# Splitting f32 weights three half units ahead, with four split buffers and three raw ones, in a one-core decoder layer

## The chip, the cores and the metric

The kernel runs on one core of a Trainium2 chip. The time is the device time of one execution in microseconds (us); the figure that counts is the median over several executions of the same kernel. The core has five engines with an instruction queue each: PE (TensorE matmul; its weight loads are listed apart as PEld), DVE (VectorE), ACT (ScalarE), POOL (GpSimd) and SP (SyncE, which here only issues transfers). They meet through semaphores. The profile gives the clock that TensorE was granted in each stretch as a share of full speed.

## What is computed

One layer of a hybrid decoder on a prompt of 2048 tokens and 8 sample tokens, width 1024, all in f32. Cut to what matters here:

```
h   = rmsnorm(x) @ w_in                     # 1024 x 3592, then two recurrent mixers side by side
o   = concat(gated_delta_net(h), mlstm(h))  # 4 + 4 heads, chunkwise, 2048 x 1024
x   = x + rmsnorm(o @ w_out)                # 1024 x 1024
u   = square(relu(rmsnorm(x) @ w_up))       # 1024 x 4096
y   = x + rmsnorm(u @ w_down)               # 4096 x 1024
```

The outputs are y for the prompt and for the sample tokens, and the states of the mixers.

## The kernel before

The prompt is worked through in four segments of 512 tokens, called 0 to 3 here; the 8 sample tokens ride with segment 1, whose tiles are therefore 520 columns wide and are multiplied in two pieces of 260. Within a segment the four weight matrices come one after another: w_in, w_o (the output projection, `w_out` above), w_up, w_dn. Each product of f32 numbers is made from three products of parts: weights and activations are each split into a high part of fewer bits and the remainder, and PE multiplies high by high (line 195), high by the activations' low part (line 196) and low by high (line 200).

A **half unit** (class `Half`, from line 155; "half" below) is one weight tile of 128 rows and 512 columns, 256 KB in HBM, that covers half of the summed dimension of one 128-wide block of outputs. For a segment's 512 columns it takes 12 matmuls. Before PE can start, the tile must be in SBUF and split:

- `load` (lines 167 to 171) takes a raw buffer, `wraw`, from a ring of four and issues the transfer on SP's queue. The buffer comes free when the subtraction of its earlier tile is done.
- `split` (lines 173 to 183) takes a buffer, `whl`, from a ring of three; ACT casts the raw tile into its first half (the high part, line 178) and DVE subtracts (line 183) to leave the low part in its second half. The buffer comes free when PE has done its last matmul on the earlier tile.
- `go` (lines 185 to 203) issues the matmuls.

There are 880 halves. In the w_o stage the columns of a segment are taken in two groups of 256, so each weight tile is loaded and split twice, and a half there is half as long on PE: 32 halves for each segment. These stages lie at about 413 to 471 us (segment 0), 1079 to 1137 (segment 1), 1716 to 1766 (segment 2) and 2193 to 2250 (segment 3).

`play` (lines 1358 to 1390) walks the list of halves. Before it issues half n it issues loads and splits that run ahead of it: all splits below n + 2, and before each split all loads below that split's number + 4. The splits are put at high priority. Between halves it lets background work run a piece at a time: the mixers (the gated delta net, its output scaling, transposes and store at lines 695 to 704, decay factors at 493 and 496; the mLSTM from line 708, decay at 730), `b_prep` (lines 1090 to 1102, which fetches the mixers' output `dO` from HBM again as `xt` and splits it into X, line 1101 on ACT, 1102 on DVE), and `norm_mid` (lines 1192 to 1220, the norm after w_o: scale with the gain at 1214, residual sum at 1215, high part of X on ACT at 1217, low part on DVE at 1218). norm_mid of a segment runs behind that segment's w_o stage, beside the matmuls of the next stage; POOL takes every second of its sums at 1215 and sums of squares at 1141. A scheduler then sets the order of each engine's queue by these priorities and by its own estimates, so a change of a number in `play` can move instructions of every engine.

Of the kernel before, what the change touches and what calls it, by code (L numbers as in the profile page):

```python
# [12 lines left out]
F32R = mybir.dt.float32r  # L13
# [11 lines left out]
def program(tc, ctx, d, T):  # L25
# [14 lines left out]
    def sb(shape, tag, bufs=1, dt=F32):  # L40
        return wk.tile(shape, dt, tag=tag, name=tag, bufs=bufs)
# [44 lines left out]
    w0 = []  # L86
    gain = const([128, 4, 8], "gain")
    for tt, tag in enumerate(("xt", "xt", "qk", "qk")):
        if tt == 2:
            Q.dma_start(gain, d["gains"])  # L90
            for i in range(2):
                w0.append(sb([128, 512], "wraw", 4))
                Q.dma_start(w0[i], d["w_gate"][:, i * 512:(i + 1) * 512])
        t = sb([128, 1040], tag, 2)
        Q.dma_start(t[:, :1024], d["x_prompt"][tt * 128:(tt + 1) * 128])
        x0.append(t)
        xs0.append(big[:, tt * 1024:(tt + 1) * 1024] if tt < 2 else sb([128, 1040], "xs", 3)[:, :1024])
# [48 lines left out]
    def tok(s, tt):  # L146
        return (tt * 128, 128) if tt < 4 else (SEG, NB)
# [9 lines left out]
    class Half:  # L157
# [9 lines left out]
        def load(self):  # L167
            if self.same is not None or self.raw is not None:
                return
            self.raw = sb([128, 512], "wraw", 4)  # L170
            Q.dma_start(self.raw, self.src)

        def split(self):
            if self.same is not None:
                self.hl = self.same.hl
                return
            self.hl = sb([128, 2, 512], "whl", 3, F32R) if self.keep is None else self.keep()
            A.copy(self.hl[:, 0], self.raw)  # L178
            raw, hi, lo = self.raw[:, :], self.hl[:, 0], self.hl[:, 1]
            if self.packed:  # L180
                raw, hi = (t.rearrange("p (a b) -> p a b", b=32)[:, :, 4:8] for t in (raw, hi))
                lo = hi
            V.tensor_tensor(lo, raw, hi.bitcast(F32), op=ALU.subtract)  # L183
# [991 lines left out]
    def pairs(src, c0, c1, tag="xt"):  # L1175

        w = c1 - c0
        k = 4 if 4 * w <= 1040 else 2

        def load(j):  # L1180
            t = sb([128, 1040], tag, 3 if tag == "xs" else 2)[:, :k * w].rearrange("p (a b) -> p a b", a=k)
            Q.dma_start(t, src[j:j + k, :, c0:c1].rearrange("j p t -> p j t"))
            return t
        ahead = load(0)
        for j in range(0, 8, k):
            t, ahead = ahead, load(j + k) if j + k < 8 else None
            yield j, k, t
# [153 lines left out]
    def step():  # L1341
        r = next(streams[0], "end")
        if r == "end":
            streams.pop(0)
            return 0.0
        return float(r or 1)
# [11 lines left out]
    def play():  # L1358
        halves = []
        for it in main:  # L1360
            h = it[0] if isinstance(it, tuple) else it
            if isinstance(h, Half) and h not in halves[-4:]:
                halves.append(h)
        place = {id(h): i for i, h in enumerate(halves)}
        loaded = split = 0
        for it in main:
            h, part = it if isinstance(it, tuple) else (it, None)
            if not isinstance(h, Half):
                it()
                continue  # L1370
            n = place[id(h)]
            while split < min(n + 2, len(halves)):
                while loaded < min(split + 4, len(halves)):
                    halves[loaded].load()
                    loaded += 1
                with tc.high_priority(300):
                    halves[split].split()
                split += 1
            while loaded < min(split + 4, len(halves)):
                halves[loaded].load()  # L1380
                loaded += 1
            h.go(part)
            if streams:
                state["due"] += h.cost() * state["rate"]
                while streams and state["due"] > 0:
                    state["due"] -= step()
            else:
                state["due"] = 0.0
# [6 lines left out]
    for group in groups(tts(0)):  # L1395
        rows = []
        for tt in group:
            n = tok(0, tt)[1]
# [115 lines left out]
    main.append(lambda: stream(final(last, 256, width(last), sumss[last], FAST, True)))  # L1514
    main.append(flush)
    play()


# [72 lines left out]
```

## Time and profile before

| | |
|---|---|
| median of 3 executions | 2653.05 us (2652.44 to 2653.79) |
| the profiled execution | 2654.11 us |
| its span in the profile | 2652.3 us |
| PE busy | 2599.9 us, 98% of the span |
| DVE, ACT, POOL busy | 1727.5, 1283.5, 433.3 us |
| moved by transfers | 377.40 MB, 142 GB/s on average |

PE is busy nearly throughout, so the time is the sum of PE's work and of the moments in which PE has nothing ready. The views that show those are the waits of PE (what ended its idle time, summed), the timeline of PE (each group of like instructions with the idle time ahead of it) and the windows (busy time, granted clock and transfer rate of a stretch).

### The profile page before, as it was taken

What the parts mean: (1) busy time and instruction counts of PE and PEld (TensorE: products, weight loads), DVE (VectorE), ACT (ScalarE), POOL (GpSimd) and SP (SyncE); (2) the same over time, 40 slices, a digit from 0 to 9 for tenths busy, and PEclk for the clock granted to TensorE, in tenths of its full rate; (3) what the DMA queues carried; (4) which work ended last, traced back from release to release, by engine and by line L of the source; (5) the groups of instructions that cost most, each with busy time, mean ns of one, the idle gap of its engine ahead of it and who ended that gap; (6) DMA issues with size and microseconds to landing.
All of it is one profiled execution on the core that took longest, in us unless ns stands there. A gap on an engine that the chain in (4) does not pass through costs nothing.

```text
span 2652.3 us, 44344 instructions
## 1 busy us (share of the span) xinstructions
PE 2599.9 (98%) x15912; PEld 2268.5 (86%) x15912; DVE 1727.5 (65%) x3513; ACT 1283.5 (48%) x3120; POOL 433.3 (16%) x494
## 2 busy tenths in 40 slices
PE   8999999999999999999999999999999999999998
PEld 6879999787888788878899999997787888788887
DVE  7665758647747656774775766577758566765445
ACT  5636557435536345653655444466354355433332
POOL 2101112311000000530100000054000003552002
PEclk9999999999999999999999999999999999999999
DMA  5444457654324345754433343455333346565222
GB/s 173 155 147 144 151 152 222 207 156 134 108 92 126 96 141 167 236 186 135 139 97 110 107 141 119 138 173 163 99 112 112 106 144 205 182 197 147 93 96 84
DMA packets 292221, 377.40 MB, mean 142 GB/s; under 512 B 42325, under 2 KB 147785, under 8 KB 291993
## 3 DMA queue, kind: packets, MB, share of 16 engines
q1 hardware_dynamic: 289312, 365.13, 44.2%
q0 software_dynamic: 2688, 9.44, 1.3%
q8 instruction: 126, 2.06, 0.3%
q14 instruction: 95, 0.77, 0.1%
HBM read 314.04 MB, written 60.53 MB: 141 GB/s over the span
## 4 chain that ended last, share of the span: by engine, by line
PE 88%; DVE 4%; DMA 4%; issue 2%; ACT 1%; POOL 0%; SPq 0%; DVEq 0%; ACTq 0%; POOLq 0%
PE bk L195 26%; PE bk L196 26%; PE bk L200 26%; DMA wraw<-w_o 1%; DVE whl L183 1%; DVE nt L1214 1%; DMA xt<-x_prompt 1%; DVE X L1218 1%; DMA xt<-dO 1%; PE mx L563 1%; PE mx L655 1%; PE mx L770 1%; PE mx L680 1%; PE mx L681 1%; PE mx L747 1%
## 5 line engine op out<-in xcount | busy, mean ns | idle before, releaser
L178 ACT CAST whl<-wraw 128x512 fp32r<-128x512 f32 x872 | 539.4, 620 | 933.7 <-PE bk L200 866.3
L183 DVE TENSOR_TENSOR whl<-wraw,whl 128x512 fp32r<-128x512 f32 (+1 forms) x872 | 636.3, 732 | 447.5 <-ACT whl L178 433.3
L195 PE MATMUL bk<-Y,whl 128*128 128x512 f32 (+2 forms) x2208 | 733.9, 347 | 4.2 <-ACT whl L178 2.0
L196 PE MATMUL bk<-Y,whl 128*128 128x512 f32 (+2 forms) x2208 | 732.1, 346 | 0.0
L195 PE MATMUL bk<-X,whl 128*128 128x512 f32 (+3 forms) x2024 | 654.9, 340 | 7.2 <-ACT whl L178 7.1
L196 PE MATMUL bk<-X,whl 128*128 128x512 f32 (+3 forms) x2024 | 653.5, 339 | 2.7 <-DVE X L1218 2.5
L200 PE MATMUL bk<-Y,whl 128*128 128x512 f32 (+2 forms) x2176 | 488.2, 344 | 6.9 <-DVE whl L183 6.9
L195 PEld LDWEIGHTS bk<-Y,whl 128*128 128x128 f32 x2208 | 416.2, 189 | 58.9 <-ACT whl L178 3.4
L196 PEld LDWEIGHTS bk<-Y,whl 128*128 128x128 f32 x2208 | 416.9, 189 | 50.4
L200 PE MATMUL bk<-X,whl 128*128 128x512 f32 (+3 forms) x2024 | 442.4, 339 | 8.9 <-DVE whl L183 8.8
L195 PEld LDWEIGHTS bk<-X,whl 128*128 128x128 f32 x2024 | 381.8, 189 | 50.5 <-ACT whl L178 9.5
L196 PEld LDWEIGHTS bk<-X,whl 128*128 128x128 f32 x2024 | 381.7, 189 | 47.5 <-DVE X L1218 4.1
L200 PEld LDWEIGHTS bk<-Y,whl 128*128 128x128 f32 x2176 | 359.1, 189 | 59.5 <-DVE whl L183 8.6
L200 PEld LDWEIGHTS bk<-X,whl 128*128 128x128 f32 x2024 | 326.3, 188 | 54.3 <-DVE whl L183 11.5
L1262 DVE TENSOR_TENSOR acc<-acc,bk 128x512 f32<-128x512 f32 (+2 forms) x296 | 164.3, 557 | 157.3 <-PE bk L200 153.4
L1141 POOL TENSOR_TENSOR NQ<-NQ,nt 128x256 f32<-128x256 f32 (+4 forms) x145 | 143.3, 991 | 470.5 <-ACT nt L1140 464.1
L1251 DVE TENSOR_TENSOR tB<-tB 128x512 f32<-128x512 f32 (+1 forms) x160 | 96.9, 608 | 44.1 <-ACT Y L1250 43.1
L305 DVE SCALAR_TENSOR_TENSOR tB<-tA,cw,tB 128x512 f32<-128x512 f32 x144 | 108.0, 750 | 13.6 <-ACT tB L301 9.3
L1252 DVE TENSOR_TENSOR Y<-tB,Y 128x512 fp32r<-128x512 f32 (+1 forms) x160 | 98.0, 615 | 3.2
L596 DVE TENSOR_TENSOR W<-xt 32x30 f32<-32x30 f32 (+14 forms) x240 | 76.2, 317 | 22.3 <-DMA xt<-dn 17.5
L1249 ACT ACTIVATE tB<-bk 128x512 f32<-128x512 f32 (+1 forms) x160 | 81.8, 511 | 16.1 <-PE bk L200 13.0
L1250 ACT ACTIVATE Y<-tB 128x512 fp32r<-128x512 f32 (+1 forms) x160 | 87.2, 549 | 4.3
(397 smaller groups left out, 2481.8 us busy)
## 6 DMA issues: line engine op xcount, KB each, us to landing
wraw<-w_dn SPq DMA_DIRECT2D x264, 256.0 KB, 2.8
wraw<-w_up SPq DMA_DIRECT2D x256, 256.0 KB, 2.8
wraw<-w_a SPq DMA_DIRECT2D x224, 256.0 KB, 2.9
wraw<-w_o SPq DMA_DIRECT2D x128, 256.0 KB, 3.3
dqkv<-tB SPq DMA_DIRECT2D x48, 256.0 KB, 3.3
gb<-drb SPq DMA_DIRECT2D x32, 256.0 KB, 3.8
qk<-dqkv SPq DMA_DIRECT2D x16, 512.0 KB, 5.7
dzo<-tB SPq DMA_DIRECT2D x32, 256.0 KB, 3.3
```

Of the source, the lines that this page charges most:

```text
L178: A.copy(self.hl[:, 0], self.raw)
L183: V.tensor_tensor(lo, raw, hi.bitcast(F32), op=ALU.subtract)
L195: PE.matmul(o, lhsT=w, rhs=acts[:, k, 0, c0:c1], start=(self.first and k == 0), stop=False)
L196: PE.matmul(o, lhsT=w, rhs=acts[:, k, 1, c0:c1], start=False, stop=(self.packed and self.last and k == 3))
L200: PE.matmul(o, lhsT=w, rhs=acts[:, k, 0, c0:c1], start=False, stop=(self.last and k == 3))
L305: V.scalar_tensor_tensor(acc, pre[:, t:t + SEG], cw[:, j, t:t + 1], acc, op0=ALU.mult, op1=ALU.add)
L1141: G.tensor_tensor(total[:, c0:c1], total[:, c0:c1], sq[:, c0:c1], op=ALU.add)
L1249: A.activation(r[:, :n], p[:, :n], AF.Relu)
L1250: A.activation(sl[:, 0, c0:c1], r[:, :n], AF.Square)
L1251: V.tensor_tensor(r[:, :n], r[:, :n], r[:, :n], op=ALU.mult)
L1252: V.tensor_tensor(sl[:, 1, c0:c1], r[:, :n], sl[:, 0, c0:c1].bitcast(F32), op=ALU.subtract)
L1262: V.tensor_tensor(a, a, p[:, :c1 - c0], op=ALU.add)
```

## The change

Three numbers change. The ring of `wraw` has three buffers instead of four, the ring of `whl` four instead of three, and `play` keeps splits below n + 3 instead of n + 2, with loads below split + 3 instead of split + 4. So the farthest load ahead of half n stays at n + 6, the farthest split goes from half n + 1 to n + 2, and the raw tiles that wait between load and split are one fewer. A raw buffer has 2 KB per partition, a split one 4 KB.

```
-                w0.append(sb([128, 512], "wraw", 4))
+                w0.append(sb([128, 512], "wraw", 3))
...
-            self.raw = sb([128, 512], "wraw", 4)
+            self.raw = sb([128, 512], "wraw", 3)
...
-            self.hl = sb([128, 2, 512], "whl", 3, F32R) if self.keep is None else self.keep()
+            self.hl = sb([128, 2, 512], "whl", 4, F32R) if self.keep is None else self.keep()
...
-            while split < min(n + 2, len(halves)):
-                while loaded < min(split + 4, len(halves)):
+            while split < min(n + 3, len(halves)):
+                while loaded < min(split + 3, len(halves)):
...
-            while loaded < min(split + 4, len(halves)):
+            while loaded < min(split + 3, len(halves)):
```

What it does to the queues is seen at two places. The first is DVE's queue behind segment 1's w_o stage, where norm_mid of segment 1 (lines 1214, 1215, 1218, 520 columns wide) stands between the subtractions of the weight tiles (line 183). Before:

```order
L183 TENSOR_TENSOR whl<-wraw,whl 128x512
L1214 SCALAR_TENSOR_TENSOR nt<-acc,gain,NQ 128x520 x3
L1218 SCALAR_TENSOR_TENSOR X_10967<-acc,gain,X_10967 128x520 x2
L1215 TENSOR_TENSOR acc<-nt,xt 128x520
L1218 SCALAR_TENSOR_TENSOR X_10967<-acc,gain,X_10967 128x520
L1214 SCALAR_TENSOR_TENSOR nt<-acc,gain,NQ 128x520
L183 TENSOR_TENSOR whl<-wraw,whl 128x512
L1218 SCALAR_TENSOR_TENSOR X_10967<-acc,gain,X_10967 128x520
L1214 SCALAR_TENSOR_TENSOR nt<-acc,gain,NQ 128x520
L183 TENSOR_TENSOR whl<-wraw,whl 128x512
L1218 SCALAR_TENSOR_TENSOR X_10968<-acc,gain,X_10968 128x520 x2
L1215 TENSOR_TENSOR acc<-nt,xt 128x520
```

And with the change:

```order
L183 TENSOR_TENSOR whl<-wraw,whl 128x512
L1214 SCALAR_TENSOR_TENSOR nt<-acc,gain,NQ 128x520 x2
L1218 SCALAR_TENSOR_TENSOR X_10970<-acc,gain,X_10970 128x520 x3
L1214 SCALAR_TENSOR_TENSOR nt<-acc,gain,NQ 128x520
L1215 TENSOR_TENSOR acc<-nt,xt 128x520
L183 TENSOR_TENSOR whl<-wraw,whl 128x512
L1218 SCALAR_TENSOR_TENSOR X_10970<-acc,gain,X_10970 128x520
L1214 SCALAR_TENSOR_TENSOR nt<-acc,gain,NQ 128x520
L183 TENSOR_TENSOR whl<-wraw,whl 128x512
L1218 SCALAR_TENSOR_TENSOR X_10971<-acc,gain,X_10971 128x520
L1215 TENSOR_TENSOR acc<-nt,xt 128x520
L1218 SCALAR_TENSOR_TENSOR X_10971<-acc,gain,X_10971 128x520
```

The runs of norm work between two subtractions stay about as long; each subtraction stands about one place further on, so the one for a given half (half 385, for instance) has 15 of the norm's operations ahead of it where it had 18.

The second place is ACT's queue at about 268 us, in segment 0's mixers, where a cast (line 178) stands ahead of the delta net's decay factors, which wait for POOL (line 496), and the next one behind them. Before:

```order
L178 CAST whl<-wraw 128x512
L345 COPY samp<-bk 128x8
L300 COPY tA<-bk 128x252
L301 ACTIVATE tB<-bk,cw 128x252
L496 ACTIVATE E<-E,iF 128x128 x4
L730 ACTIVATE gb<-gb,mp_112 128x128
L178 CAST whl<-wraw 128x512
L730 ACTIVATE gb<-gb,mp_112 128x128 x3
```

And with the change:

```order
L178 CAST whl<-wraw 128x512
L345 COPY samp<-bk 128x8
L300 COPY tA<-bk 128x252
L301 ACTIVATE tB<-bk,cw 128x252
L331 ACTIVATE tB<-bk 128x260
L496 ACTIVATE E<-E,iF 128x128 x4
L178 CAST whl<-wraw 128x512
L730 ACTIVATE gb<-gb,mp_112 128x128 x4
```

The rows read nearly alike, but the cast ahead of line 496 is that of half 77 instead of half 76, and the one behind it that of half 78 instead of 77.

Two more facts of the order are used below. In segment 3 the rows of DVE around its last L703 are the same word for word, each subtraction belonging to the next half. And in segment 0's w_o stage PE meets the last four transposes of the mixers' output (line 702) six halves later, in half 128 instead of 122, so that five halves instead of ten stand between them and the first matmul (half 133) that reads the columns of X made from them.

## Rows read from the trace of the kernel before

**Rows 1.** The page: the span, and busy time of each engine.

```profile
span 2652.3 us, 44344 instructions
...
PE 2599.9 (98%) x15912; PEld 2268.5 (86%) x15912; DVE 1727.5 (65%) x3513; ACT 1283.5 (48%) x3120; POOL 433.3 (16%) x494
```

**Rows 2.** Waits of PE: line waited for, us in total, times, longest us.

```profile
PE bk L200 <- DVE whl L183: 15.7, 14, 2.7
PE bk L195 <- ACT whl L178: 9.1, 12, 1.4
```

**Rows 3.** Timeline of PE: start us, us, group, [idle before, who ended it].

```profile
268.33 0.39 PE L195 MATMUL bk<-Y,whl 128*128 128x260 f32 x1 [1.35 <-ACT whl L178]
...
501.36 1.19 PE L200 MATMUL bk<-Y,whl 128*128 128x512 f32 x4 [1.03 <-DVE whl L183]
...
507.03 1.20 PE L200 MATMUL bk<-Y,whl 128*128 128x512 f32 x4 [2.62 <-DVE whl L183]
...
1173.82 1.54 PE L200 MATMUL bk<-Y,whl 128*128 128x512 f32 x4 [2.69 <-DVE whl L183]
...
1759.83 0.74 PE L200 MATMUL bk<-X,whl 128*128 128x256 f32 x4 [1.43 <-DVE whl L183]
...
2200.47 0.75 PE L200 MATMUL bk<-X,whl 128*128 128x256 f32 x4 [2.63 <-DVE whl L183]
```

**Rows 4.** Timeline of ACT at 268 us.

```profile
266.20 1.28 ACT L496 ACTIVATE E<-E,iF 128x128 f32<-128x128 f32 x4 [5.02 <-POOL E L493]
267.68 0.60 ACT L178 CAST whl<-wraw 128x512 fp32r<-128x512 f32 x1
```

**Rows 5.** Timeline of DVE in norm_mid of segment 1.

```profile
1163.67 0.75 DVE L1214 SCALAR_TENSOR_TENSOR nt<-acc,gain,NQ 128x520 f32<-128x520 f32 x1
1164.94 1.80 DVE L1218 SCALAR_TENSOR_TENSOR X<-acc,gain,X 128x520 fp32r<-128x520 f32 x1
...
1173.08 0.68 DVE L183 TENSOR_TENSOR whl<-wraw,whl 128x512 fp32r<-128x512 f32 x1
```

**Rows 6.** Timeline of DVE in segment 3's w_o stage.

```profile
2199.07 0.75 DVE L703 SCALAR_TENSOR_TENSOR on<-mx,ghalf,on 128x512 f32<-128x512 f32 x1 [4.85 <-DMA wraw<-w_o]
2199.73 1.89 DVE L183 TENSOR_TENSOR whl<-wraw,whl 128x512 fp32r<-128x512 f32 x3
```

**Rows 7.** Window: us, busy PE, PEld, DVE, ACT, POOL; clock, DMA share, GB/s.

```profile
1170.00:1180.00 10.00, 7.13 (x24) 4.87 (x23) 9.59 (x8) 6.14 (x12) 7.69 (x6) 0.83 0.45 141
```

**Rows 8.** Timeline of ACT, then DVE, in segment 2's w_o stage, undisturbed.

```profile
1723.27 0.62 ACT L178 CAST whl<-wraw 128x512 fp32r<-128x512 f32 x1 [0.23 <-PE bk L200]
1724.67 0.62 ACT L178 CAST whl<-wraw 128x512 fp32r<-128x512 f32 x1 [0.78 <-PE bk L200]
...
1723.92 0.69 DVE L183 TENSOR_TENSOR whl<-wraw,whl 128x512 fp32r<-128x512 f32 x1 [0.71 <-ACT whl L178]
```

**Rows 9.** Windows of the w_o stages of segments 0, 1 and 3 (columns as rows 7).

```profile
413.00:471.00 58.00, 56.30 (x480) 55.35 (x479) 48.70 (x140) 43.04 (x120) 14.99 (x18) 1.00 0.74 226
1079.00:1137.00 58.00, 53.05 (x427) 51.08 (x426) 46.87 (x74) 39.77 (x91) 30.90 (x35) 1.00 0.78 250
...
2193.00:2250.00 57.00, 50.39 (x398) 48.72 (x397) 36.49 (x55) 33.36 (x79) 18.18 (x20) 0.97 0.71 212
```

**Rows 10.** Tile `wraw`, issue to landing, in the windows of rows 9, in order.

```profile
DMA to landing us min/median/max: 3.2/4.5/4.9
...
DMA to landing us min/median/max: 3.3/5.0/6.1
...
DMA to landing us min/median/max: 2.8/3.6/5.4
```

**Rows 11.** Waits of ACT for late weight tiles (columns as rows 2).

```profile
ACT whl L178 <- DMA wraw<-w_o: 24.0, 14, 3.6
```

**Rows 12.** Timeline of DVE, end of segment 0's mixers.

```profile
426.29 0.75 DVE L703 SCALAR_TENSOR_TENSOR on<-mx,ghalf,on 128x512 f32<-128x512 f32 x1 [0.47 <-PE mx L702]
...
434.12 0.69 DVE L1102 TENSOR_TENSOR X<-xt,X 128x512 fp32r<-128x512 f32 x1 [1.13 <-ACT X L1101]
```

## Prediction

> **What bounds the kernel now.** The page comes first: PE is busy for 2599.9 of the span's 2652.3 us [rows 1], so at most 52.4 us can be had from anything but less work on PE. The waits of PE come next, since the change touches one thing on PE's side, how early a split tile is ready: 15.7 us for the low parts from DVE and 9.1 us for the high parts from ACT, 24.8 us together [rows 2]. The rest of PE's idle time waits for norms and other matters that stay. The timeline of PE then shows where the 24.8 us lie [rows 3]: few and long stalls, not many short ones. Those I price are at 268 us (segment 0's mixers), 501 and 507 us (norm_mid of segment 0), 1174 us (norm_mid of segment 1), 1760 us (norm_mid of segment 2; one like it, 1.44 us, stands at 2244 us in segment 3), and 2200 us. All profiled figures belong to the execution of 2654.11 us, 1.8 us longer than its span and 1.06 us above the median of 2653.05; I take the sum off the median. A difference under 0.2%, 5.3 us, can't be told from none.
>
> **Why these stalls can shrink.** In each, the tile had long been in SBUF and its split stood behind something else on the queue of ACT or DVE. At 268 us the cast stood behind the decay factors, which had waited 5.02 us for POOL, and began at 267.68 [rows 4]. In norm_mid of segment 1 the subtraction began at 1173.08, behind a run of the norm's operations that take 1.80 us where the like of them take 0.75 in other moments [rows 5], and PE's next matmul on a low part began at 1173.82. At 2200 us DVE stood 4.85 us, in front of the scaling at L703, and then did three subtractions in a row [rows 6]. The change doesn't shorten these queues; it moves each split one half further ahead of PE, so PE has one half more to work on when the queue stops. A half's worth is 1.40 us at 256 columns, which is the step from one cast to the next where nothing disturbs [rows 8], and twice that, 2.8 us, at 512.
>
> **The gains.** Each stall can shrink by at most itself or one half's worth, and by nothing if the queue's delay grows with the lead. The stall at 268: 1.35 us, under one half's 2.8, and the cast that stood behind L496 now stands ahead of it: -1.35 (0 to -1.35). At 501 and 507, 1.03 + 2.62 = 3.65 us is one delay met twice: -2.0 (0 to -2.8), since DVE's queue carries the same work either way. At 1174, 2.69 us: -2.4 (0 to -2.7). At 1760 and 2244, 1.43 and 1.44 us, halves now of 256 columns and then 512: -1.0 each, -2.0 (0 to -2.8). At 2200, 2.63 us against 1.40: -1.3 (0 to -1.4). Sum -9.05 (0 to -11.1). The other waits in the 24.8 us (at the start, and short ones in the w_o stages, behind transfers) I leave as they are.
>
> **The clock.** Behind three of these stalls, at 507, 1174 and 2200 us, the granted clock averages 0.83 over 10 us; the window behind the second stands for the three [rows 7]. That is 3.4 us at 1.2 instead of 2.4 GHz, and every such dip costs 0.17 x 10 = 1.7 us of PE's work on top of the stall. A dip that follows a stall may go when the stall shrinks. I take two of three, as the gains above leave 0.3 us of the stall at 1174, 1.3 of that at 2200 and 1.65 of the pair at 501 and 507: -3.4 (0 to -5.1).
>
> **The price: three raw buffers.** A raw buffer is held from the issue of its load to the end of its subtraction: landing, then cast and subtraction, which undisturbed take from 1723.27 to 1723.92 + 0.69, 1.34 us [rows 8]; I take 1.4 with the reissue. With landing L, four buffers feed a half each (L + 1.4)/4 us, three (L + 1.4)/3. In w_a, w_up and w_dn a half takes PE 2.8 us, three of them 8.4 us, well over any landing seen, so the ring costs nothing there. The w_o stages are the place, with halves of 256 columns; there SP issues as soon as a buffer is freed. From rows 9 and 10, by the median landing:
>
> - segment 0: (4.5 + 1.4)/3 = 1.97 us against the stage's pace of 58/32 = 1.81: 32 x 0.16 = +5.1
> - segment 1: (5.0 + 1.4)/3 = 2.13 against 1.81: 32 x 0.32 = +10.2
> - segment 3: (3.6 + 1.4)/3 = 1.67 against 57/32 = 1.78: nothing; segment 2, whose landings are shorter, nothing either.
>
> With four buffers the same four sums give 1.48, 1.60 and 1.25, always under the pace. So the upper bound is +15.3. The lower is 0: the three split tiles ahead of PE absorb late ones, and where the mixers' own matmuls stand between the halves a late tile costs nothing. Which lies nearer? ACT already waits 24.0 us for late w_o tiles [rows 11], while all of PE's waits for ACT's casts are 9.1 us [rows 2]: 0.38 of the lateness at most comes through. 0.38 x 15.3 = **+5.8**.
>
> **The moved transposes.** In segment 0 PE meets the mixers' last four transposes six halves later, so five halves instead of ten lie between them and the first matmul that reads X made from them. From L703 to the end of X's low part took 426.29 to 434.81, 8.5 us [rows 12], by way of a store and a fetch. Five halves of 256 columns are 5 x 1.40 = 7.0 us and about 0.7 for the transposes; 0.8 us is missing: **+1.0** (0 to +2.8, if the landings there lengthen by 2 us). The other moves that the order shows (norm_mid of segment 0 begins two halves earlier on PE, the norm before the mixers some halves earlier or later) keep their distance in time to what they feed, and I cost them at nothing.
>
> **The sum.** -9.05 - 3.4 + 5.8 + 1.0 = -5.65, so 2653.05 - 5.65 = **2647.4 us**.
>
> **The rivals.**
>
> 1. Fewer transfers in flight land sooner. In the w_o stages with four loads outstanding the landing is 4.5 and 5.0 us at 226 and 250 GB/s, and 3.6 at 212 [rows 9, 10]. If the time in the queue falls with the number outstanding, L falls by a quarter to 3.4 and 3.75 us, three buffers give 1.6 and 1.72 us, under the pace of 1.81, and the ring's price falls to about +1; with it the +1.0 of the transposes: -9.05 - 3.4 + 1.0 = -11.45, 2641.6 us. For it: landings as short as 2.8 us in the same stages. Against it: the mixers' and norms' own transfers share these stretches and stay. The Trainium skill, "DMA: Bandwidth & Descriptors", section "Latency and other measured facts", has it that a lighter load on HBM makes the fixed cost of a transfer smaller; the three rows, longer landings at higher rates, agree in direction.
>
> 2. DVE is the bound in norm_mid of segments 0 and 1, and a lead of one half is eaten in the stretch. In segment 1 DVE is busy 9.59 us of 10 there and POOL 7.69 [rows 7], and the same operation takes 1.80 instead of 0.75 us [rows 5]. Then the stalls and the dips at 507 and 1174 stay where they were: 2.0 + 2.4 and two thirds of the 3.4, 6.7 us, don't come, and -5.65 + 6.7 = +1.05: 2654.1 us, no difference. Against it: the order shows the subtraction of half 385 behind 15 of the norm's operations instead of 18, at up to 1.8 us each. The Trainium skill, "SBUF — State Buffer", section "SBUF: two separate sides", says that an operation of VectorE with two inputs in SBUF and one of GpSimd that reads SBUF hold a shared port in turn and block each other wholly; the row of 1.80 beside one of 0.75 fits that, and by it the subtraction itself, with two such inputs, may be blocked wherever it is put.
>
> 3. Slower: the ring of three becomes the bound of the w_o stages of segments 0 and 1. It decides there once L stays above 3 x 1.81 - 1.4 = 4.0 us, which both medians do [rows 10]. Then the full +15.3 comes, with +1.0 for the transposes, and the new stalls bring dips of the clock that use up what the old ones gave: -9.05 + 15.3 + 1.0 = +7.25, 2660.3 us. For it: segment 1 already has PE busy for 53.05 of 58 us [rows 9] and a landing of up to 6.1. Against it: the landing was measured with four in flight, and in the pace of 1.81 is room of the mixers.
>
> That the change doesn't do what it says is no case of its own: the order shows every split one half further on.
>
> **How the numbers follow.** The forecast 0.45, its own range 2641 to 2651; since its middle lies just beyond 5.3 us, 0.30 of it count as faster and 0.15 as the same. Rival 1 0.18, faster. Rival 2 0.20, the same. Rival 3 0.17, of which 0.01 ends within the bound. So faster 0.48, the same 0.36, slower 0.16. The range reaches from 2637, rival 1 with the stalls at their lower bounds and all three dips gone (-11.1 - 5.1 = -16.2), to 2660, where rival 3 lies.
>
> **What would show it.** Right: PE's waits for the two split lines fall from 24.8 to about 16 us; the idle time ahead of PE's matmuls at 268 us is gone, at 507, 1174 and 2200 us it is under 1.4 us; of the three windows at 0.83 one is left. The price shows in ACT's wait for late w_o tiles, which rises from 24.0 us to about 40, and in the w_o stages of segments 0 and 1, about 2 and 4 us longer than 58. Rival 1 shows as landings of `wraw` under 4 us in these two stages, rival 2 as the same 2.6 us stalls at the same places, rival 3 as stalls of PE behind ACT's casts every few halves of these stages. The prediction is wrong if the stages of w_o don't lengthen and the time doesn't fall, for then the gains were mis-sized; or if the time falls by more than 16 us.

## The result, and the profile after

The change made the kernel slower: a median of 2671.17 us (2670.0 to 2677.98, 4 runs) against 2652.74 us, a ratio of 1.0069 with a 95% interval of 1.0056 to 1.0081. The forecast was 2647.4, and the range ended at 2660. The slower rival, the ring of three raw buffers as the bound of the w_o stages, was right about the mechanism and about half of the place (it named segments 0 and 1, and segments 2 and 3 paid as much), and too small. Medians and ratios in this document leave out three executions of over 4200 us, in which the granted clock was 0.56 to 0.88.

The page of the changed kernel, and under it PE's waits (line waited for: us in total, times, longest us):

```profile
span 2668.3 us, 44329 instructions
...
PE 2609.2 (98%) x15912; PEld 2278.2 (85%) x15912; DVE 1728.9 (65%) x3513; ACT 1281.5 (48%) x3120; POOL 431.6 (16%) x494
```

```profile
PE bk L195 <- ACT whl L178: 15.1, 14, 2.4
PE bk L200 <- DVE whl L183: 9.5, 8, 2.1
```

Read against [rows 1, 2], the two waits together have not moved (24.6 us, 24.8 before) but have changed sides: the wait for low parts fell from 15.7 to 9.5, that for high parts rose from 9.1 to 15.1. The span grew by 16.0 us. PE's idle time (span less busy) went from 52.4 to 59.1, +6.7 us, and its busy time from 2599.9 to 2609.2, +9.3 us, with the same 15912 matmuls. So more than half of the loss is not waiting at all: the same matmuls took longer. The windows show why (columns as [rows 7]):

```profile
445.00:455.00 10.00, 9.01 (x63) 8.54 (x63) 7.64 (x26) 6.33 (x16) 2.36 (x3) 0.83 0.72 235
475.00:485.00 10.00, 7.88 (x26) 5.83 (x26) 5.75 (x14) 6.77 (x18) 2.90 (x3) 0.66 0.57 173
1122.00:1132.00 10.00, 7.80 (x53) 7.59 (x52) 6.47 (x13) 8.25 (x19) 1.86 (x3) 0.83 0.73 246
2258.00:2268.00 10.00, 8.02 (x36) 7.46 (x37) 6.73 (x10) 5.69 (x16) 6.89 (x9) 0.66 0.89 294
```

These are four of eight such windows; the others, at 1097, 1768, 1860 and 2210 us, read 0.83 like the first. A window at 0.83 holds one dip to 1.2 GHz, 1.7 us lost as in [rows 7], one at 0.66 two. That is ten dips. The kernel before has four, the three of the prediction and one at 1850 us behind a wait that the change doesn't touch. Six more dips at 1.7 us are 10.2 us, about the 9.3 by which PE's busy time grew. This is no accident of one execution: the mean granted clock of the change's four executions was 0.991 to 0.994, that of E1 below, which has nine dips fewer in its trace, 0.996 to 0.997 in five.

Where the waiting moved is on ACT (waits of ACT, columns as [rows 11]):

```profile
ACT whl L178 <- PE bk L200: 761.0, 468, 4.3
ACT whl L178 <- DMA wraw<-w_o: 57.9, 50, 6.2
...
ACT whl L178 <- DMA wraw<-w_dn: 41.2, 24, 4.6
...
ACT whl L178 <- DMA wraw<-w_a: 22.7, 16, 4.2
```

The row of [rows 11], 24.0 us in 14 waits, is now 57.9 in 50; those for w_dn and w_a were 1.9 and 2.1 us and are 41.2 and 22.7. ACT used to wait for PE to free a split buffer (866.3 us, now 761.0), which is the healthy order: the raw tile lies ready. Now it waits for the tile. The windows of the four w_o stages, each from its first matmul to the next stage's, to a microsecond:

```profile
409.00:478.00 69.00, 61.91 (x498) 59.52 (x496) 50.15 (x143) 46.49 (x134) 19.01 (x19) 0.98 0.69 197
1087.00:1149.00 62.00, 55.76 (x431) 54.39 (x430) 46.91 (x74) 39.51 (x91) 32.35 (x36) 0.94 0.73 232
1724.00:1776.00 52.00, 48.21 (x394) 47.60 (x393) 34.43 (x52) 31.59 (x74) 17.87 (x21) 0.97 0.57 181
2204.00:2266.00 62.00, 52.69 (x395) 50.90 (x394) 36.90 (x55) 32.55 (x77) 19.13 (x22) 0.92 0.68 203
```

Against [rows 9] the stages of segments 0, 1 and 3 are longer, move less per second (197, 232 and 203 GB/s where it was 226, 250 and 212) and run at a lower clock. All four together are 22.1 us longer than before (table below). The rest of the layer is 6.1 us shorter: above all the w_in stage of segment 1, beside the mixers (217.05 us before, 212.78 now), and the stretch behind segment 1's w_o stage, beside norm_mid (172.17, now 168.22). One turn of the ring, in segment 0, read in the timelines of DVE, SP (queue of loads), ACT and PE:

```profile
463.25 0.68 DVE L183 TENSOR_TENSOR whl<-wraw,whl 128x512 fp32r<-128x512 f32 x1
465.86 0.69 DVE L183 TENSOR_TENSOR whl<-wraw,whl 128x512 fp32r<-128x512 f32 x1 [0.34 <-ACT whl L178]
...
463.96 0.33 SPq L171 DMA_DIRECT2D wraw<-w_o  x1
466.58 0.33 SPq L171 DMA_DIRECT2D wraw<-w_o  x1
...
469.33 0.62 ACT L178 CAST whl<-wraw 128x512 fp32r<-128x512 f32 x1 [0.17 <-DMA wraw<-w_o]
...
470.13 0.68 DVE L183 TENSOR_TENSOR whl<-wraw,whl 128x512 fp32r<-128x512 f32 x1
...
472.57 0.39 PE L195 MATMUL bk<-X,whl 128*128 128x256 f32 x1 [0.56 <-ACT whl L178]
```

A subtraction ends at 463.93 and frees a raw buffer; the load goes out at 463.96; its cast waits for the landing and begins at 469.33; its subtraction ends at 470.81, when the buffer is free again. That is 6.9 us for a turn in which three halves pass, 2.3 us each, and PE needs 1.40 for one. The next load, 466.58, is again 0.03 us behind the subtraction that ended at 466.55. PE stands 0.56 us for the next half. That is little because other matmuls fill the time: in the whole of segment 0's stage (409 to 478 us) PE waits 2.1 us for casts.

```profile
PE bk L195 <- ACT whl L178: 2.1, 4, 0.8
```

### The profile page after: what moved, and what is told of

Read it like the earlier page. It is cut to its first block, busy times and chain, and to the rows that moved or that the text cites. A ratio compares the mean times of both kernels' runs of the same rounds, so it can differ in the third digit from the quotient of the medians.

```text
span 2668.3 us, 44329 instructions
## 1 busy us (share of the span) xinstructions
PE 2609.2 (98%) x15912; PEld 2278.2 (85%) x15912; DVE 1728.9 (65%) x3513; ACT 1281.5 (48%) x3120; POOL 431.6 (16%) x494
## 4 chain that ended last, share of the span: by engine, by line
PE 85%; DMA 6%; DVE 5%; ACT 2%; issue 1%; POOL 0%; SPq 0%; DVEq 0%; ACTq 0%; POOLq 0%
PE bk L195 25%; PE bk L196 25%; PE bk L200 25%; DMA wraw<-w_o 3%; DVE whl L183 2%; DVE X L1218 1%; ACT whl L178 1%; DMA xt<-x_prompt 1%; PE mx L563 1%; DVE nt L1214 1%; DMA xt<-dO 1%; PE mx L655 1%; PE mx L681 1%; PE mx L680 1%; PE mx L672 1%
## 5 line engine op out<-in xcount | busy, mean ns | idle before, releaser
L178 ACT CAST whl<-wraw 128x512 fp32r<-128x512 f32 x872 | 539.0, 619 | 927.0 <-PE bk L200 761.0
L200 PEld LDWEIGHTS bk<-Y,whl 128*128 128x128 f32 x2176 | 359.4, 189 | 56.4 <-DVE whl L183 5.8
```

Of the source, the lines that this page charges most:

```text
L200: PE.matmul(o, lhsT=w, rhs=acts[:, k, 0, c0:c1], start=False, stop=(self.last and k == 3))
```

## The experiments

The lengths of the four w_o stages in the traces (us, first matmul of the stage to first matmul of the next), with span and PE's busy time, for the kernel before, the change and the four experiments that separate the rings:

| | before | change | E1: 4 raw, 4 split | E3: 3 raw, 3 split | E5: 4th raw for w_o only | E6: 2 raw, 4 split |
|---|---|---|---|---|---|---|
| segment 0 | 57.6 | 68.5 | 64.4 | 67.2 | 66.1 | 85.8 |
| segment 1 | 58.4 | 61.9 | 57.0 | 64.7 | 57.5 | 82.1 |
| segment 2 | 49.8 | 52.0 | 48.4 | 54.1 | 48.4 | 65.3 |
| segment 3 | 56.9 | 62.4 | 54.1 | 65.0 | 53.5 | 79.2 |
| sum | 222.7 | 244.8 | 223.9 | 251.0 | 225.5 | 312.4 |
| span | 2652.3 | 2668.3 | 2640.7 | 2694.5 | 2656.4 | 2764.3 |
| PE busy | 2599.9 | 2609.2 | 2592.9 | 2615.2 | 2598.7 | 2637.7 |

The numbers in `play` play no part. A kernel with four raw and three split buffers and the change's limits n + 3 and split + 3 has every queue in the same order as the kernel before, and one with the change's rings and the old limits has the change's order. So of the edits of the change only the two ring sizes act.

**E1, four raw and four split buffers.** Both rings at four need 1.1 KB more than a partition has left. The mLSTM state, kept in two buffers, is updated in place, and one tile is cut to what is used of it:

```
-                w0.append(sb([128, 512], "wraw", 3))
+                w0.append(sb([128, 512], "wraw", 4))
...
-            self.raw = sb([128, 512], "wraw", 3)
+            self.raw = sb([128, 512], "wraw", 4)
...
-        Cn = sb([128, 2, 130], "C", 2)
+        Cn = Cp
...
-            C0 = sb([128, 2, 130], "C", 2)
+            C0 = sb([128, 2, 130], "C", 1)
...
-            t = sb([128, 1040], "qk", 2)[:, :1024].rearrange("p (a b) -> p a b", a=8)
+            t = sb([128, 1024], "qk", 2).rearrange("p (a b) -> p a b", a=8)
```

> Four raw buffers beside the four split ones; to make room the mLSTM state is updated in place and a tile is cut from 1040 to 1024 columns. Theory A (the ring of three raw buffers sets the pace of the w_o stages, 32 x hold / 3, where the hold is the time from a load's issue to the end of its subtraction): the four w_o stages fall back from 68.5, 61.9, 52.0 and 62.4 us to within 2 us of 57.6, 58.4, 49.8 and 56.9, the gains outside of them stay (about 2 us by the start of the first, 4 us in norm_mid of segments 0 and 1 each), and the time is about 2645 us. Theory B (what costs is the new order of the queues, which the fourth split buffer brings): the stages of segments 0 and 3 stay over 64 and 60 us and the time over 2662.

Measured: 2643.88 us against 2656.08 for the kernel before on the same chip, a ratio of 0.9951 (0.9933 to 0.9968): faster than both kernels. Its page, PE's waits, ACT's wait and the windows of three w_o stages:

```profile
PE 2592.9 (98%) x15912; PEld 2264.5 (86%) x15912; DVE 1731.3 (66%) x3513; ACT 1280.4 (48%) x3120; POOL 435.5 (16%) x494
```

```profile
PE bk L200 <- DVE whl L183: 8.6, 11, 1.6
...
PE bk L195 <- ACT whl L178: 5.2, 6, 1.6
```

```profile
ACT whl L178 <- DMA wraw<-w_o: 22.1, 16, 4.0
```

```profile
407.00:471.00 64.00, 59.75 (x490) 57.06 (x488) 49.93 (x143) 47.21 (x136) 18.18 (x19) 1.00 0.69 209
1077.00:1134.00 57.00, 52.36 (x428) 51.00 (x427) 47.41 (x73) 39.67 (x91) 30.53 (x35) 1.00 0.78 256
...
2185.00:2239.00 54.00, 48.27 (x397) 46.85 (x395) 34.50 (x53) 31.68 (x75) 16.88 (x19) 1.00 0.70 213
```

PE's waits for split tiles are 13.8 us instead of 24.6, ACT's wait for w_o is back at 22.1, three stages are shorter than before the change, and the clock is full in all of them; of the ten dips one is left, at about 1845 us. Against the change the span is 27.6 us shorter: 16.3 of busy time (nine dips, 15.3) and 11.3 of idle time. That is what the missing raw buffer costs between these two traces. Of the 27.6 us, 20.9 lie in the w_o stages (4.2, 4.9, 3.7 and 8.3), 3.4 in the two dips right behind segment 0's stage, and 2.5 before the ninth half, where executions differ by more than that (see the end). Not every one of the nine dips need be the ring's. Five come at waits of PE for a split tile; the one at 447 us comes behind 1.65 us for X and 0.76 for a cast, the two at 478 us behind 1.97 us for the next norm (line 250), and the one at 1099 us at 2.38 us for POOL, a wait that E1 has too (2.37 us at 1088 us), without a dip.

Segment 0's stage stays at 64.4 us, 6.8 over the kernel before, so theory B has the larger part there. PE is busy for 59.75 of 64 us, where [rows 9] has 56.30 of 58: more work, and some more idle time. The new order moves 16 of the mixers' matmuls (lines 702 to 746) into this stage, out of the w_in stage ahead of it, which is 4.1 us shorter (212.98 us).

**E2, the control.** The kernel before with only the room-making edits of E1.

> The kernel before with only the room-making edits of the first run (state in place, narrower tile). Both theories: 2653 us within 2; if it is off by more, the first run is read against this one and not against the kernel before.

Measured: 2657.77 against 2656.08 us, a ratio of 1.0002 (0.9989 to 1.0015). The edits cost nothing that can be measured, so E1's gain is the fourth split buffer's: 11.6 us in the traces against the kernel before, 14.1 against this control (span 2654.8). Its w_o stages (59.3, 59.2, 49.9 and 56.4 us) differ from those before by up to 1.7, so a difference under 2 us in one stage says nothing.

**E3, three raw buffers with three split ones.** The raw ring alone is taken from four to three (`"wraw", 3`, loads below split + 3).

> Three raw buffers, three split ones, splits as far ahead as before. Theory A: the w_o stages are as long as with the change, 66, 62, 53 and 61 us within 3, the stalls of about 2.6 us at 507 and 1174 us stay, and the time is 2670 to 2676. Theory B: the stages as before, 58, 58, 50 and 57, and 2653 to 2658.

Measured: 2692.47 us, a ratio of 1.0133 (1.0113 to 1.0153). PE's waits and ACT's:

```profile
PE bk L195 <- ACT whl L178: 30.3, 21, 5.1
PE bk L200 <- DVE whl L183: 16.8, 13, 2.7
```

```profile
ACT whl L178 <- DMA wraw<-w_o: 47.3, 38, 4.8
```

Worse than theory A said: the span grew by 42.2 us, 28.3 of them in the w_o stages and 6.2 before the ninth half. The wait for low parts stays at 16.8 us, as before the change, since the split ring is the old one; the wait for high parts is three times the old. With E1 the four corners agree: at four raw buffers the fourth split one gains 11.6 us of span, at three it gains 26.2; at four split buffers the fourth raw one gains 27.6, at three 42.2.

**E4, five raw buffers with three split ones**, the same memory as the change (`"wraw", 5`, loads below split + 5).

> Five raw buffers, three split ones: the same memory as the change, given to the other ring. Theory A: the hold over five is far under the pace, so only loads that land late in the kernel before gain: the stages shorten by 0 to 2 us each, the stalls in the norms stay, 2648 to 2653. Theory B: no difference beyond 2 us unless the order moves.

Measured: 2657.72 us, a ratio of 1.0006 (0.9995 to 1.0016). No gain; its w_o stages sum to 220.4 us. Four raw buffers were enough for three split ones; the spare 2 KB is worth something only in the split ring, and only if it isn't taken from the raw one.

**E5, the fourth raw buffer for w_o alone.** E1 with three buffers in the ring and one more that only the second half of every odd w_o block takes:

```
-            self.raw = sb([128, 512], "wraw", 4)
+            self.raw = sb([128, 512], "wrawo", 1) if self.fourth else sb([128, 512], "wraw", 3)
...
-                us += unit(d["w_o"][j], lambda: halves, [cols], lambda parts, j=j: evac(j, parts))
+                us += unit(d["w_o"][j], lambda: halves, [cols], lambda parts, j=j: evac(j, parts)); us[-1].fourth = j % 2 == 1
```

> The first run's kernel, but its fourth raw buffer serves w_o tiles alone (every fourth of them); all other tiles go through three. Theory A (three raw buffers bind in the w_o stages and hardly elsewhere): it keeps all but 2 to 4 us of what the first run gained, that is 6 to 11 us faster than the kernel before. Rival C (three also bind where a half takes 2.8 us, or the start is what costs): no faster than the kernel before.

Measured: 2655.16 us against 2656.30, a ratio of 0.9993 (0.9983 to 1.0002). The stages are E1's, but for 1.7 us in segment 0 (table), so in them theory A holds; the time is not, as rival C had it. Of the 15.7 us of span between E5 and E1, 5.9 lie before the ninth half and 6.6 in the norms behind the w_o stages of segments 0 and 1. The timeline of DVE in norm_mid of segment 1 shows what happens there:

```profile
1169.69 0.68 DVE L183 TENSOR_TENSOR whl<-wraw,whl 128x512 fp32r<-128x512 f32 x1
...
1179.16 1.79 DVE L183 TENSOR_TENSOR whl<-wraw,whl 128x512 fp32r<-128x512 f32 x1
1180.87 3.54 DVE L1218 SCALAR_TENSOR_TENSOR X<-acc,gain,X 128x520 fp32r<-128x520 f32 x2
1184.33 4.08 DVE L183 TENSOR_TENSOR whl<-wraw,whl 128x512 fp32r<-128x512 f32 x3
```

The subtraction at 1169.69 is that of half 384 and frees the raw buffer for half 387, whose load goes out at 1172.02. In E1 that load went out at 1153.86, for a buffer one place further back, its cast stood at 1163.97 instead of 1180.96, and its subtraction directly behind that of half 386; here two of the norm's operations, 3.54 us, stand between. PE stands 2.09 us for half 387. So here a ring of three let a late subtraction hold back the load, the cast and the next subtraction too. That it does so in general isn't shown: the stretch behind segment 1's w_o stage takes 167.8 us in E1 and 171.7 in E5, but 168.2 in the change, which has three raw buffers for everything, and 169.5 in E6 with two.

**E6, two raw buffers with four split ones** (`"wraw", 2`, loads below split + 2).

> The change with two raw buffers instead of three (loads below split + 2). Theory A: the tile's hold of 5 to 6 us, over two buffers, is 2.5 to 3 us a half: the w_o stages take 32 x 2.75 = 88 us each, some 100 us more than with the change in all four, and as a half of the wide stages takes 2.8 us they only begin to be touched: 2760 to 2850 us. Rival B (the order of the queues costs, not the ring): under 2690.

Measured: 2766.46 us, a ratio of 1.0419 (1.0404 to 1.0434), at the lower end of theory A and far from B. The waits of ACT, and the windows of the w_o stages of segments 0 and 1:

```profile
ACT whl L178 <- DMA wraw<-w_o: 108.2, 82, 7.5
ACT whl L178 <- DMA wraw<-w_dn: 89.1, 51, 7.8
```

```profile
410.00:496.00 86.00, 68.14 (x495) 63.95 (x494) 51.34 (x149) 49.79 (x140) 14.28 (x19) 0.92 0.57 158
1109.00:1191.00 82.00, 59.76 (x432) 54.22 (x431) 44.00 (x73) 41.26 (x91) 28.17 (x35) 0.98 0.57 182
```

Of the 112.0 us by which the span exceeds that of the kernel before, 89.7 are in the four stages. They move 158 and 182 GB/s, where E1 moves 209 and 256: it isn't the memory that is short, it is the tiles allowed in flight. The runs line up by the number of raw buffers: with four split buffers the four stages sum to 312.4, 244.8 and 223.9 us at two, three and four raw ones, with three split buffers to 251.0, 222.7 and 220.4 at three, four and five.

**E7 and E8, w_o in one pass**, with three and with four raw buffers. Each w_o tile is loaded and split once and multiplied with both column groups, so a half is 2.8 us long there too:

```
-        for cols in tok_halves(s):
-            us = []
...
-                us += unit(d["w_o"][j], lambda: halves, [cols], lambda parts, j=j: evac(j, parts))
-            out.append(us)
-        return out
+            us += unit(d["w_o"][j], lambda: halves, tok_halves(s), lambda parts, j=j: evac(j, parts))
+        return [us, []]
...
-        main.append(flush if s == 0 else (lambda: None))
+        main.append(flush)
```

> The change, with w_o in one pass: each w_o tile is loaded and split once and multiplied with both column groups, so a w_o half takes 2.8 us and there are 16 instead of 32 in a segment. Only the difference to the next run counts. Theory A: 3 x 2.8 = 8.4 us is over any hold, so three raw buffers cost at most 8 us against four, where they cost 27 with two passes. Rival C (the traffic of these stages binds, whatever the length of a half): over 15 us.

> The first run's kernel (four raw, four split) with w_o in one pass. Theory A: at most 8 us faster than the run with three. Against the kernel before either way: half as many w_o loads and casts, but the first product waits for all 512 columns; 2635 to 2665 us.

Measured: 2702.85 and 2694.87 us, 8.0 apart in the medians and 4.6 in the spans, at theory A's limit of 8 and far below the 27 with two passes. The w_o stages themselves are 1.7 us apart (236.1 and 234.4 in sum), where those of the change and E1 are 20.9 apart. ACT's wait for w_o is 6.5 us with three buffers, 57.9 in the change:

```profile
ACT whl L178 <- DMA wraw<-w_o: 6.5, 2, 5.4
```

So three raw buffers are short where a half is 1.40 us. One pass also halves the loads of w_o, so these two runs alone don't tell the length of a half from the traffic; that the traffic doesn't bind rests on E6 and E1 (182 and 256 GB/s in the same stage). Both are over the 2635 to 2665 us I expected and slower than the kernel before (ratios 1.0181 and 1.0152): with nothing to run beside the norms PE stands 21.4 us, in two waits, for POOL's sums in the norm behind w_o. One pass is no way out.

## Why the prediction was wrong

- **The gains.** Their sum was near, but only once the raw ring is back, and then in part by luck: -9.05 for the stalls and -3.4 for the clock, -12.45 together, against -11.6 us of span from the kernel before to E1. Of these 7.0 are busy time (three dips fewer) and only 4.6 idle time, since PE's waits for split tiles fell by 11.0 us while other waits grew. In the change itself the gains came in part. The stall at 268 us is gone. In norm_mid of segment 1 the 2.69 us became 0.47 + 0.31, -1.9 where -2.4 was priced. In segment 0 the pair of 1.03 + 2.62 became 1.57 + 2.00: nothing of the -2.0 came, as rival 2 had it for this place, though the dip behind it went. Two of the three dips went, as priced; the one at 2200 stayed. The stalls at 1760 and 2244 did not shrink, and 2.63 us at 2200 became 2.09:

```profile
515.45 1.20 PE L200 MATMUL bk<-Y,whl 128*128 128x512 f32 x4 [1.57 <-DVE whl L183]
520.51 1.20 PE L200 MATMUL bk<-Y,whl 128*128 128x512 f32 x4 [2.00 <-DVE whl L183]
...
1186.73 0.50 PE L195 MATMUL bk<-Y,whl 128*128 128x512 f32 x1 [0.47 <-ACT whl L178]
1189.16 1.20 PE L200 MATMUL bk<-Y,whl 128*128 128x512 f32 x4 [0.31 <-DVE whl L183]
...
1771.72 0.58 PE L195 MATMUL bk<-X,whl 128*128 128x256 f32 x1 [1.84 <-ACT whl L178]
...
2211.58 0.93 PE L200 MATMUL bk<-X,whl 128*128 128x256 f32 x4 [2.09 <-DVE whl L183]
...
2260.72 0.58 PE L195 MATMUL bk<-X,whl 128*128 128x256 f32 x1 [1.83 <-ACT whl L178]
```

- **The price of the ring: the step that failed.** "0.38 x 15.3 = +5.8" measured 27.6 us (E1 against the change), 11.3 of idle time and 16.3 of busy time. Two errors are in it. First, the waits that the ring would bring were too few. The stages' pace of 1.81 and 1.78 us holds stalls and other work; between them PE takes a half in 1.40 us. So segment 3 was costed at nothing, because 1.67 us a half was under 1.78, but 1.67 is over 1.40; against E1 it lost 8.3 us, and segment 2, also costed at nothing, 3.7, together more than segments 0 and 1 (4.2 and 4.9). ACT's waits for w_o rose from 24.0 to 57.9 us, not to about 40. The factor 0.38 was not the error: from E1 to the change these waits rise by 35.8 us and PE's waits for split tiles by 10.8, a share of 0.30. Second, every stall that the ring brought was priced as a stall, without the dip of the clock. I had counted dips on the side of the gains only; nine dips, 15.3 us, are more than half of the 27.6. The wide stages were put at nothing too, and in the change that held: ACT waits 41.2 and 22.7 us for w_dn and w_a there, but behind segment 1's w_o stage the change is only 0.4 us longer than E1. E5 leaves it open for other orders.

- **The hold.** The estimate landing + 1.4 gave 5.9, 6.4 and 5.0 us in segments 0, 1 and 3; the medians from issue to end of subtraction in the change are 6.2, 5.8 and 5.7 (5.0 in segment 2). The sum was near, its parts were not. Landings did shorten, as rival 1 had it. The trace of the change has none on record, but E3, also with three raw buffers, has 6 to 9 in each stage; in segments 0, 1 and 3:

```profile
DMA to landing us min/median/max: 2.6/3.0/5.2
...
DMA to landing us min/median/max: 2.7/3.2/5.6
...
DMA to landing us min/median/max: 2.7/2.9/6.3
```

[rows 10] has 4.5, 5.0 and 3.6, from 4 to 5 landings on record among some 30 loads of each stage, a thin base. In the change a cast that waited for its tile began 3.6, 3.5, 3.1 and 3.2 us behind the issue in segments 0 to 3 (medians of 11 to 15 halves in a stage), and its subtraction ended some 1.35 us later, as priced. Over all halves the rest of the hold is 1.9 to 2.5 us, as many casts had other work of ACT or a split buffer to wait for. So rival 1's mechanism was at work, and did not keep the ring from binding. (Its sum also counts only one of its two terms of +1.)

- **The transposes.** +1.0 for segment 0: PE stood 1.65 us for X behind them, once; near enough as a stall, but a dip followed at 447 us. In E1 the same wait is 0.21 us, so these 3.4 us are among the 27.6.

- **Rival 3** gave 2660 from the full ring price and the dips used up. It was the case that came, about 11 us short, for the two reasons above.

## What to carry to other kernels

A ring's size is to be set by the turn time (issue, landing, and the queues of every engine that must touch the tile before it is free) over the buffers. Compare it with the time in which the consumer takes one tile in the stage with the shortest tiles, and not only with that stage's mean. Here 1.48 and 1.60 us (four raw buffers), little over 1.40, left nothing for a fifth buffer to gain; 1.67 was under the mean of 1.78 and still cost 8.3 us. And where TensorE's clock falls behind a stall, price a new stall with its dip, just as a removed one.

## What was not expected of the hardware

- In the kernel before, the change and E1 every dip costs 1.7 us, or twice that, but not every stall brings one. 1.57 and 2.00 us at 515 and 520 us, 5 us apart, brought none (the window from 512 to 522 us reads 1.00), and neither did 2.41 us at 2227; single stalls of 2.20 us at 1125 and of 2.09 at 2212 did. The same wait for POOL brought one in the change (2.38 us) and none in E1 (2.37 us). The condition was not looked for.

- A subtraction of 128x512 takes 0.69 us undisturbed [rows 8] and 1.79 us at 1179 us in E5, while POOL sums squares for the norm (line 1141, 1176.91 to 1180.40). The Trainium skill, "SBUF — State Buffer", section "SBUF: two separate sides", says that such an operation, with two inputs in SBUF, and one of GpSimd that reads SBUF block each other for a whole instruction. The two durations agree with it.

- Fewer loads in flight land sooner: medians of 2.9 to 3.2 us with three raw buffers (E3) against 3.6 to 5.0 with four, in segments 0, 1 and 3. This agrees in direction with what "DMA: Bandwidth & Descriptors" of the Trainium skill says in "Latency and other measured facts" on a lighter load. What of it is fewer loads of weights and what the slower stage isn't separated.

Left open: what sets the time before the ninth half, 5.9 us longer in E5 than in E1. The cast of half 4 begins there at 23.75 us in E1 and at 31.25 in E5. The ring is not shown to be the cause: E8, whose queues are E1's up to there, takes 44.5 us for this stretch where E1 takes 39.3, and the change takes 41.7, E5 45.1, E6 with two raw buffers 42.4. Without this stretch E5 and E1 are 9.8 us apart; by the medians, each against its own kernel before, they are 11.1 apart. Nor was an order held fixed while a ring changed, since the ring sizes set the order.
